# Moving three side tasks of a two-block transformer kernel: weight sums, modulation columns, first values

## The chip, the cores and the metric

The kernel runs on one core of a Trainium2 chip. The metric is the device time of one launch in microseconds (us); the time of a kernel is the median of several runs. The core's engines each run their own instruction queue in order: PE (matrix products), DVE (vector), ACT (scalar, activations), POOL (a second vector engine) and SP (which here only issues DMAs). DMAs are issued from SP's queue and from POOL's queue.

## The reference, cut to what matters

Two blocks over 1024 tokens of 1024 features, all in float32. The first block is attention followed by a feed-forward with a convolution; the second is a gated linear attention over a context of 256 tokens and then the 1024 tokens, followed by an MLP. Both are modulated or normed:

```python
# first block
mix = token_mixer(x, w_in, b_forget, rel_bias, w_out)      # 8 forgetting + 8 band heads
x = layer_norm(ALPHA * x + mix, ln1_g, ln1_b)
u = causal_conv3(x @ w_up) + conv_b                         # 2 x 2816 columns
value, gate = split(u)
ffn = (value * gelu(gate)) @ w_down                         # 2816 -> 1024
x = layer_norm(ALPHA * x + ffn, ln2_g, ln2_b)
# second block, with six modulation vectors of 1024 from c @ ada_w + ada_b:
#   0 shift1, 1 scale1, 2 gate1, 3 shift2, 4 scale2, 5 gate2
h   = modulate(rmsnorm(x, g1), shift1, scale1)
x   = x + gate1 * gla_mixer(context, h)                     # 4 heads, both directions
h   = modulate(rmsnorm(x, g2), shift2, scale2)
x   = x + gate2 * (relu(h @ w1) ** 2) @ w2                  # MLP, 4096 wide
out = rmsnorm(x, g3)
```

## The kernel before, in words

**Products.** A float32 product is three PE matmuls (`mm3`): high by high, high by low, low by high. The two halves of an operand come from `split`: a cast on ACT, then a subtraction on DVE. The large products (the two up and the two down products) use seven block products in place of eight (Strassen-Winograd), so some operands are sums of blocks. The sums of the weights `w_down` are made in `right_sums`: for each of 11 groups it loads two tiles of 512 KB (`sumw`, `sumv`), does four DVE operations of 128x512, and stores both tiles to DRAM (T1T3w, T4T2w). The down pass loads them back as operands.

**Stages, in order of time.** Attention (0 to some 480 us, `attention_phase`); the product with `w_out` and the first norm (`mixed`, to 642); the first up pass with convolution and gate (`up_pass`, `conv_gate`, 642 to 1063, 22 pairs of column blocks); the down pass (`ffn_down`, 1063 to 1352), into which the context's part of the second block (`context`) is mixed; the last norms of the first block and the values of the first head (`norm1`, `first_values`, 1352 to 1400); the gated linear attention (`prepare` and `scan` of four heads, 1400 to 1708); its output gate (`gate_out`, 1708 to 1797); output product, second up pass, second down pass (to 2558).

**What sets the order.** The generators are interleaved by `merge`: it always advances the one that has spent the smallest share of its stated total. From that program order and from priorities (the transposes have a high one) a scheduler fixes each engine's order when the kernel is built; nothing is reordered on the chip. In the attention `merge` mixes the modulation vectors 0 and 1, `down_sums` (all of `right_sums`, with loads and stores on SP's queue) and the attention itself. In the down pass it mixes `most()`, the six first of the seven block products (one step is 12 matmuls), and `context`.

**Modulation.** `ada(v, c, 256, ...)` makes 256 columns of vector v: eight weight tiles of 128 KB (`ada_w`) are loaded, scaled and added on DVE (one operation each, into `ada_acc`), and a matmul sums over the partitions. For v = 2 and 5 the result is stored to DRAM; for v = 3 and 4 it stays. Before, the four vectors 2 to 5 are made in the gated linear attention, 36 steps after each scan, with the weights in the same four buffers (`raw`) through which `w_get` brings the weights of the products.

**Convolution and gate.** `conv_gate` runs after each pair of the up pass: ACT scales the block, DVE adds two shifted copies (L1063, L1064), ACT does the gelu, DVE multiplies. Every second pair it also makes the sums of the left operand of the down pass. The next pair's ACT copy of a block product (L801) overwrites what L1064 has read, and PE reuses the PSUM bank after that copy.

**Scan.** `scan(h)` is a chain over eight tiles: PE makes `att`, `dS` and three `o` matmuls; DVE forms the new state (`Snew`) and, with the root mean square from ACT and POOL, normalises `o` into `res` (L1318), which frees the one bank of `o`. `gate_out` is 768 matmuls (`tokp`) of 128x256.

Of the kernel before, what the change touches and what calls it, by code (L numbers as in the profile page):

```python
# [10 lines left out]
F32 = mybir.dt.float32  # L11
# [6 lines left out]
P = 128  # L18
D = 1024
# [19 lines left out]
def drain(gen):  # L39
    for _ in gen:  # L40
        pass
# [13 lines left out]
def build(tc, I, out, dbg=None, stop=None):  # L55
# [4 lines left out]
    def pool(stack, name, bufs, **kw):  # L60
        return stack.enter_context(tc.tile_pool(name=name, bufs=bufs, **kw))
# [128 lines left out]
    def right_sums(W, n, pl, dst, load, store):  # L190

        w, v = (pl.tile([P, D], F32, tag=x, name=f"sum{x}") for x in "wv")
        for i, t in enumerate((w, v)):
            load.dma_start(out=t.rearrange("p (h c) -> p h c", h=2), in_=W[2 * n + i].rearrange("h p c -> p h c"))
        yield 1
        DVE.tensor_tensor(out=w[:, XS], in0=w[:, YS], in1=w[:, XS], op=ALU.subtract)
        DVE.tensor_tensor(out=w[:, YS], in0=v[:, YS], in1=w[:, YS], op=ALU.subtract)
        yield 1
        DVE.tensor_tensor(out=v[:, YS], in0=v[:, YS], in1=w[:, XS], op=ALU.subtract)
        DVE.tensor_tensor(out=v[:, XS], in0=v[:, XS], in1=v[:, YS], op=ALU.subtract)  # L200
        yield 1
        for x, t in zip(dst, (w, v)):
            store.dma_start(out=x[n], in_=t)
# [8 lines left out]
    def attention_phase():  # L212
# [7 lines left out]
        pp = pool(st, "pp", 5)  # L220
        f1 = pool(st, "f1", 1)
        ar = pool(st, "ar0", 2)
        twp = pool(st, "tw", 1)

        Wqk, Wv = wlist("wqk"), wlist("wv")
        Wv0 = wlist("wv0")
# [315 lines left out]
                except StopIteration:  # L542
                    return

        def down_sums():

            for n in range(NCH // 2):
                yield from right_sums(I["w_down"], n, twp, TW, SP, SP)

        tws = down_sums()  # L550

        def split_y(p):
            kk = (p + 4) % 8
            for c in (slice(0, 512), slice(512, T)):
# [12 lines left out]

        for p in range(8):
            feed[0] = projections(p)
            merge([(some(mod, 13), 13), (some(tws, 5), 5), (until_pair(), attn_cost(p)), (feed[0], 20801 * ((p % 2 == 0) + (p < 7)) + 1), (split_ys(p), 6)])  # L570
        return st

    st = attention_phase()
# [478 lines left out]
    def conv_weights(st):  # L1052
        convc.append(pool(st, "convc", 1, reuse_waits="tile").tile([P, 2 * NCH, 4], F32, name="convc"))
        SP.dma_start(out=convc[0], in_=I["conv"])
        convc.append(pool(st, "sums1", 2, reuse_waits="tile"))

    def conv_gate(n, gv_, gg_, *_):

        o = res[3], res[7]
        for i, (psum, x) in enumerate(zip((gv_, gg_), o)):  # L1060
            c = convc[0][:, 2 * n + i, :]
            ACT.activation(x, psum, AF.Identity, scale=c[:, 2:3], bias=c[:, 3:4])
            DVE.scalar_tensor_tensor(out=x[:, 1:T], in0=psum[:, 0:T - 1], scalar=c[:, 1:2], in1=x[:, 1:T], op0=ALU.mult, op1=ALU.add)  # L1063
            DVE.scalar_tensor_tensor(out=x[:, 2:T], in0=psum[:, 0:T - 2], scalar=c[:, 0:1], in1=x[:, 2:T], op0=ALU.mult, op1=ALU.add)  # L1064
        gelu = ACT.activation(o[1], o[1], AF.Gelu_apprx_tanh)
        if n == NCH - 1:
            exp_tables(gelu)
        if n % 2 == 0:
            even[:] = [convc[1].tile([P, T], F32, tag="g", name="geven")]
            DVE.tensor_tensor(out=even[0], in0=o[0], in1=o[1], op=ALU.mult)  # L1070
            return
        DVE.tensor_tensor(out=o[0], in0=o[0], in1=o[1], op=ALU.mult)
        a, b = convc[1].tile([P, D], F32, tag="s12", name="sums12"), convc[1].tile([P, 512], F32, tag="s4", name="sums4")
        left_sums(even[0], o[0], a, b)
        for x, t in (("A12A22", o[0]), ("A11S3", even[0]), ("S1S2", a)):
            POOL.dma_start(out=left1[x][n // 2], in_=t)
        POOL.dma_start(out=narrow1["S4"][n // 2], in_=b)
# [43 lines left out]
    def ffn_down():  # L1121

        nonlocal hi, lo, rawp, wp
        st, cst = ExitStack(), ExitStack()
        set_banks(st, "f", {"mm": (1, 5, "down"), "c": (1, 2, "z hps fp tokp xtp"), "ct": (1, 1, "ctp ktp dS xtp")}, reuse_waits="tile")
        counts = ("r0", 2), ("l0", 2), ("draw1", 4), ("l1", 4), ("r1", 4), ("rp", 2), ("fc1", 1)
        r0, l0, raw, l1, r1, rp, fc = (pool(st, n, b, reuse_waits="tile") for n, b in counts)
        left, right = in_turn((l0, 2), (l1, 4)), in_turn((r0, 2), (r1, 4))
        rawp, wp = (pool(cst, n, 4, side="right") for n in ("wraw1", "wsplit1"))
        B = blocks(wlist("w_down"), left1, narrow1, TW)  # L1130
        gb = [fc.tile([P, D], F32, name=f"ln2{c}") for c in "gb"]
        junk = fc.tile([P, D], BF16, name="junk")
        mv = [fc.tile([P, 6], F32, name=f"mvd{t}") for t in range(NT)]

        def with_x1(t, c, of):

            x = rp.tile([P, 512], F32, tag="x", name="x1res")
            SP.dma_start(out=x, in_=x1d[t][:, c])
            DVE.scalar_tensor_tensor(out=res[t][:, c], in0=x, scalar=ALPHA, in1=of, op0=ALU.mult, op1=ALU.add)

        def add(o, a, b):
            DVE.tensor_tensor(out=o, in0=a, in1=b, op=ALU.add)

        def complete(t, c, psum):
            i = 0 if c == XS else 1
            add_sum(res[t][:, c], psum, res[t][:, c], mv[t][:, i:i + 1])

        def normed(t):
            layer_norm(res[t], mv[t], *gb, junk)
            SP.dma_start(out=x2d[t], in_=res[t])  # L1150

        def p1(t, p):
            ACT.copy(res[t][:, XS], p)

        def p6(t, p):
            add(res[t + 4][:, XS], p, res[t][:, XS])
            with_x1(t, XS, res[t][:, XS])

        def p2(t, p):
            complete(t, XS, p)  # L1160

        def p5(t, p):
            add(res[t + 4][:, YS], p, res[t + 4][:, XS])
            with_x1(t, YS, res[t + 4][:, YS])
            with_x1(t + 4, YS, res[t + 4][:, YS])

        def p3(t, p):
            complete(t, YS, p)
            with_x1(t + 4, XS, res[t + 4][:, XS])
            normed(t)  # L1170

        def p7(t, p):
            complete(t + 4, YS, p)
            add(res[t + 4][:, XS], p, res[t + 4][:, XS])

        def p4(t, p):
            complete(t + 4, XS, p)
            normed(t + 4)

        def run(a, b, evac, by_tile):  # L1180
            psums = [acc("down") for _ in range(4)]
            for t in block_product(B, raw, left, right, NCH // 2, psums, a, b, by_tile, mm3):
                if t is not None:
                    evac(t, psums[t])
                yield t

        def most():
            for a, b, f in (("A11", "B11", p1), ("S2", "T2", p6), ("A12", "B21", p2), ("S1", "T1", p5), ("S4", "B22", p3), ("S3", "T3", p7)):
                for t in run(a, b, f, 3):
                    yield 2724 if t is None else 2043  # L1190
                if f is p2:
                    bcast(gb[0], "ln2_g")
                    bcast(gb[1], "ln2_b")

        def norm1(t):
            rows(res[t], t, vec["gs1"], vec["sh1"], rms_of(res[t], junk), rp)
            split(by_k(res[t]), hi[:, :, toks(t)], lo[:, :, toks(t)])

        def first_values():

            for t, psum in token_product(Wgv0, hi, lo, NT, HV + 32):
                ACT.copy(v0[t], psum[:, 0:HV])
                DVE.tensor_copy(out=ht[t], in_=psum[:, HV:HV + 32])
                yield

        merge([(most(), 179784), (context(cst), CTXSHARE)])
        cst.close()
        actp = pool(act_st, "act2", 1, side="right")
        rawp, wp = pool(st, "wraw2", 4), pool(st, "wsplit2", 4)
        hi, lo = (actp.tile([P, KD, T], F32R, name=n) for n in ("act2_hi", "act2_lo"))  # L1210
        values = first_values()
        ready = deque(range(4))
        for t in run("A22", "T4", p4, 3):
            if ready:
                norm1(ready.popleft())
        for t in range(4, NT):
            norm1(t)
        drain(values)
        st.close()
# [107 lines left out]
    ac = pool(gla_st, "ac", 1)  # L1327

    def modulation():
        for v in (2, 4, 3, 5):  # L1330
            for c in range(0, D, 256):
                yield from ada(v, c, 256, None, ac)

# [2 lines left out]
    for h in range(4):  # L1336
        scan(h)
        if h < 3:
            prepare(h + 1)
        for _ in range(36):  # L1340
            next(mod, None)
    for h in range(4):
        gate_out(h)
# [270 lines left out]
```

## Time and profile before

| | us |
|---|---|
| median of 3 runs (2556.66 to 2559.73) | 2557.68 |
| the profiled execution | 2559.18 |
| its span in the trace | 2557.5 |
| PE busy | 2425.3 (95%) |
| DVE busy | 1744.9 (68%) |
| ACT busy | 1260.3 (49%) |

How to read it: the span is the trace's time from the first to the last instruction; the profiled execution is 1.7 us longer than its span and 1.5 us longer than the median. PE is busy nearly all the time, so the time that can be had lies in the stages where it is not, and the tables of stages below show which these are. A granted clock of 1.00 is full speed of PE (2.4 GHz), and PE at its lower level runs at half of that.

### The profile page before, as it was taken

The page shows a single profiled execution, that of the slowest core. Times are in us where ns is not written, and L with a number is a line of the kernel's source. Part 1 is how long each engine was busy: PE and PEld are TensorE (multiplying, and loading weights), DVE is VectorE, ACT ScalarE, POOL GpSimd, SP SyncE. Part 2 cuts the span into 40 slices and gives each one's busy share as a digit, 9 for nine tenths or more (in the row PEclk, how much of TensorE's full clock was granted, in tenths as well). Part 3 has the DMA queues.
Part 4 walks back from the last instruction along what each step waited for, and adds up shares of the span by engine and source line. Part 5 has one row for each costly group of instructions (what it writes and reads, how often), then busy time and mean ns, then how long its engine had stood idle before and what let it go on. Part 6 is the DMA issues. An engine that isn't in the chain of part 4 may idle for free. (4 is left out here: it accounts for less than half of the span.)

```text
span 2557.5 us, 37112 instructions
## 1 busy us (share of the span) xinstructions
PE 2425.3 (95%) x12822; PEld 2066.3 (81%) x12822; DVE 1744.9 (68%) x3299; ACT 1260.3 (49%) x2284; POOL 445.6 (17%) x677
## 2 busy tenths in 40 slices
PE   8999999998999999899997989979999999999998
PEld 7788989777888888678887878869788878878886
DVE  6876666658788888667585876652578777555456
ACT  4555556735555554565364543322355555544443
POOL 4675742421000000100022000000011111100000
PEclk9989999999999999899999999989999999999999
DMA  8653322353223322476652222231436777576565
GB/s 281 228 183 96 98 84 60 98 168 111 90 87 116 108 90 95 148 239 199 200 184 76 64 88 88 63 122 34 148 124 226 276 271 273 202 240 209 196 208 189
DMA packets 189085, 387.24 MB, mean 151 GB/s; under 512 B 22296, under 2 KB 54680, under 8 KB 188896
## 3 DMA queue, kind: packets, MB, share of 16 engines
q1 hardware_dynamic: 168032, 310.14, 37.0%
q0 software_dynamic: 20864, 74.72, 7.9%
q8 instruction: 101, 1.65, 0.3%
q14 instruction: 88, 0.72, 0.1%
HBM read 275.95 MB, written 100.43 MB: 147 GB/s over the span
## 5 line engine op out<-in xcount | busy, mean ns | idle before, releaser
L103 DVE TENSOR_TENSOR dpart<-draw,dpart 128x512 fp32r<-128x512 f32 x378 | 250.6, 693 | 183.2 <-ACT dpart L102 175.9
L102 ACT CAST dpart<-draw 128x512 fp32r<-128x512 f32 x378 | 221.5, 620 | 243.5 <-PE Y L131 65.7
L130 PE MATMUL s<-act_hi,uh 128*128 128x512 f32 (+1 forms) x640 | 244.0, 381 | 1.0 <-ACT res L805 1.0
L131 PE MATMUL s<-act_lo,uh 128*128 128x512 f32 (+1 forms) x640 | 243.3, 380 | 0.0
L132 PE MATMUL s<-act_hi,ul 128*128 128x512 f32 (+1 forms) x640 | 243.2, 380 | 0.0
L601 POOL TENSOR_TENSOR rstd<-rstd,mhalf 128x1 f32<-128x1 f32 x74 | 54.8, 744 | 926.7 <-DVE rstd L600 734.4
L130 PE MATMUL tokp<-wh,act_hi 128*128 128x256 f32 (+1 forms) x512 | 148.3, 292 | 0.0
L394 ACT ACTIVATE P<-P,mx 128x640 f32<-128x640 f32 (+7 forms) x128 | 94.4, 738 | 108.9 <-DVE mx L391 86.6
L132 PE MATMUL tokp<-wh,act_lo 128*128 128x256 f32 (+1 forms) x512 | 147.6, 289 | 0.0
L131 PE MATMUL tokp<-wl,act_hi 128*128 128x256 f32 (+1 forms) x512 | 147.2, 289 | 0.0
L130 PEld LDWEIGHTS s<-act_hi,uh 128*128 128x128 f32 x640 | 121.7, 190 | 24.1 <-ACT res L805 1.5
L131 PEld LDWEIGHTS s<-act_lo,uh 128*128 128x128 f32 x640 | 121.7, 190 | 22.2
L132 PEld LDWEIGHTS s<-act_hi,ul 128*128 128x128 f32 x640 | 121.5, 190 | 22.4
L396 POOL TENSOR_SCALAR P<-P,mx 128x640 f32<-128x640 f32 (+7 forms) x128 | 94.7, 743 | 183.2 <-DVE mx L395 166.5
L130 PE MATMUL s<-ext_8hi,uh 128*128 128x512 f32 (+1 forms) x320 | 121.2, 379 | 1.4 <-ACT res L809 1.4
L131 PE MATMUL down<-dpart 128*128 128x512 f32 x308 | 121.7, 396 | 0.4 <-DVE dpart L103 0.2
L131 PE MATMUL s<-ext_8lo,uh 128*128 128x512 f32 (+1 forms) x320 | 121.2, 379 | 0.6 <-DVE ext_8lo L103 0.6
L132 PE MATMUL s<-ext_8hi,ul 128*128 128x512 f32 (+1 forms) x320 | 121.1, 378 | 0.0
L132 PE MATMUL down<-dpart 128*128 128x512 f32 x308 | 120.9, 393 | 0.0
L102 ACT CAST uh<-res 128x1024 fp32r<-128x1024 f32 x80 | 83.0, 1040 | 77.0 <-PE s L131 61.4
L130 PE MATMUL down<-dpart 128*128 128x512 f32 x308 | 117.7, 395 | 2.2 <-ACT dpart L102 2.2
L103 DVE TENSOR_TENSOR ul<-res,uh 128x1024 fp32r<-128x1024 f32 x80 | 96.5, 1207 | 26.5 <-ACT uh L102 26.1
(373 smaller groups left out, 7174.9 us busy)
## 6 DMA issues: line engine op xcount, KB each, us to landing
ada_w<-in_ada_w SPq DMA_DIRECT2D x192, 128.0 KB, 2.2
res<-in_w_up SPq DMA_DIRECT2D x44, 512.0 KB, 3.3
res<-in_mlp_w SPq DMA_DIRECT2D x32, 512.0 KB, 4.3
draw<-in_mlp_w SPq DMA_DIRECT2D x48, 256.0 KB, 3.7
draw<-in_w_down SPq DMA_DIRECT2D x33, 256.0 KB, 3.3
raw<-in_wqk SPq DMA_DIRECT2D x32, 256.0 KB, 3.4
sumw<-in_mlp_w SPq DMA_DIRECT2D x16, 512.0 KB, 6.6
sumv<-in_mlp_w SPq DMA_DIRECT2D x16, 512.0 KB, 6.6
```

The source lines that it names most:

```text
L102: ACT.copy(h, raw)
L103: DVE.tensor_tensor(out=l, in0=raw, in1=h, op=ALU.subtract)
L130: PE.matmul(out=o, lhsT=ah, rhs=bh, start=first, stop=False, **kw)
L131: PE.matmul(out=o, lhsT=ah, rhs=bl, start=False, stop=False, **kw)
L132: return PE.matmul(out=o, lhsT=al, rhs=bh, start=False, stop=last, **kw)
L394: ACT.activation(Pm[:, 0:W], Pm[:, 0:W], AF.Exp, bias=mx[:, 0:1], scale=-1.0, accum_out=mx[:, 1:2])
L396: POOL.tensor_scalar(out=Pm[:, 0:W], in0=Pm[:, 0:W], scalar1=mx[:, 2:3], scalar2=0.0, op0=ALU.mult, op1=ALU.add)
L601: POOL.tensor_tensor(out=t[:, 1:2], in0=t[:, 0:1], in1=mhalf, op=ALU.pow)
```

## The change

It touches six places.

A. `down_sums` and its pool are taken out of the attention.

B. The same sums are made in the first up pass: `conv_gate` calls `right_sums` at every even pair, 11 times, placed behind the pair's last load. Loads are on SP's queue, stores on POOL's. The pool for them has one buffer, and the old pool of two buffers is split into two pools of one.

C. The six first steps of `most()` are taken before the context is mixed in; the stated total of the rest is smaller by the same.

D. Modulation vectors 2 and 5 are made in the down pass, as a third generator, with two buffers of their own for the weights; their matmul uses the bank of the context's transposes ("ct").

E. A step of `first_values` (24 matmuls) is taken before each of the last four norms.

F. In the gated linear attention only vectors 4 and 3 remain, with 18 steps after each scan in place of 36.

```diff
@@ attention_phase
-        def down_sums():
-            for n in range(NCH // 2):
-                yield from right_sums(I["w_down"], n, twp, TW, SP, SP)
-        tws = down_sums()
...
-            merge([(some(mod, 13), 13), (some(tws, 5), 5), (until_pair(), attn_cost(p)), (feed[0], 20801 * ((p % 2 == 0) + (p < 7)) + 1), (split_ys(p), 6)])
+            merge([(some(mod, 13), 13), (until_pair(), attn_cost(p)), (feed[0], 20801 * ((p % 2 == 0) + (p < 7)) + 1), (split_ys(p), 6)])
@@ conv_weights, conv_gate
-        convc.append(pool(st, "sums1", 2, reuse_waits="tile"))
-
-    def conv_gate(n, gv_, gg_, *_):
+        convc.extend(pool(st, n, b, reuse_waits="tile") for n, b in (("even1", 1), ("sums1", 1)))
+
+    def conv_gate(n, gv_, gg_, last):
...
         if n % 2 == 0:
+            with tc.issue_after(last.ins):
+                drain(right_sums(I["w_down"], n // 2, convc[2], TW, SP, POOL))
             even[:] = [convc[1].tile([P, T], F32, tag="g", name="geven")]
@@ ffn_down
-        set_banks(st, "f", {"mm": (1, 5, "down"), "c": (1, 2, "z hps fp tokp xtp"), "ct": (1, 1, "ctp ktp dS xtp")}, reuse_waits="tile")
+        set_banks(st, "f", {"mm": (1, 5, "down"), "c": (1, 2, "z hps fp tokp xtp"), "ct": (1, 1, "ctp ktp dS ada xtp")}, reuse_waits="tile")
...
+        ar, ac = pool(cst, "ar", 2, side="right"), pool(cst, "ac", 1, side="right")
...
-        merge([(most(), 179784), (context(cst), CTXSHARE)])
+        def modulation():
+            for v in (2, 5):
+                for c in range(0, D, 256):
+                    yield from ada(v, c, 256, ar, ac)
+
+        products = most()
+        for _ in range(6):
+            next(products)
+        merge([(products, 163440), (context(cst), CTXSHARE), (modulation(), 72)])
...
         for t in range(4, NT):
+            next(values)
             norm1(t)
@@ gated linear attention
-            for v in (2, 4, 3, 5):
+            for v in (4, 3):
...
-        for _ in range(36):
+        for _ in range(18):
             next(mod, None)
```

What this does to the order on the engines, at three places.

DVE around the first pair of the up pass, after the change. L103 are the splits whose results (`act_lo`, `ext_4lo`, `ext_8lo`, `ul`) PE reads; L704 to L708 form the blocks to split; L1022 and L1024 end a norm; L196 to L200 are the weight sums.

```order
L103 TENSOR_TENSOR act_lo<-res_6921,act_hi 128x8x128
L707 TENSOR_TENSOR res_6920<-res_6920,t_7721 128x512
L103 TENSOR_TENSOR ext_4lo<-t_7721,ext_4hi 128x4x128
L196 TENSOR_TENSOR sumw<-sumw 128x512
L103 TENSOR_TENSOR act_lo<-res_6924,act_hi 128x8x128
L103 TENSOR_TENSOR ext_8lo<-res_6920,ext_8hi 128x8x128
L704 TENSOR_TENSOR res_6921<-res_6925,res_6921 128x512
L705 TENSOR_TENSOR t_7826<-res_6925,res_6921 128x512
L708 TENSOR_TENSOR res_6925<-res_6925 128x512
L197 TENSOR_TENSOR sumw<-sumv,sumw 128x512
```

The same place before (the lines of that code are 8 higher there: L712 is L704).

```order
L103 TENSOR_TENSOR act_lo<-res_7035,act_hi 128x8x128
L715 TENSOR_TENSOR res_7034<-res_7034,t_7835 128x512
L103 TENSOR_TENSOR ext_4lo<-t_7835,ext_4hi 128x4x128
L103 TENSOR_TENSOR act_lo<-res_7038,act_hi 128x8x128
L103 TENSOR_TENSOR ext_8lo<-res_7034,ext_8hi 128x8x128
L712 TENSOR_TENSOR res_7035<-res_7039,res_7035 128x512
L713 TENSOR_TENSOR t_7940<-res_7039,res_7035 128x512
```

The rows of after are the second of two whole sums that stand here; the first one's four operations stand in the eleven rows ahead. So eight operations on loaded tiles now stand among the splits of the first pair.

ACT at the start of the down pass, after the change. `dpart` are the casts of the down product's operands, `wh` those of the context's weights, `ctx_x` and `ctx_f` the context's norm and modulation, between which PE transposes (`ctp`).

```order
L614 ACTIVATE ctx_f,ss<-ctx_x 128x1024
L102 CAST wh<-raw 128x576 x2
L102 CAST dpart<-draw 128x512 x2
L935 ACTIVATE ctx_x<-ctx_x,rstd 128x1024
L1057 ACTIVATE res_6925<-res_6925 128x1024
L86 ACT_TABLE_LOAD
L102 CAST wh<-raw 128x576
L631 ACTIVATE ctx_f<-ctp,v_shc,v_gsc 128x128 x4
L102 CAST wh<-raw 128x576 x4
L631 ACTIVATE ctx_f<-ctp,v_shc,v_gsc 128x128 x4
L102 CAST wh<-raw 128x576
L102 CAST dpart<-draw 128x512
```

The same place before.

```order
L622 ACTIVATE ctx_f,ss<-ctx_x 128x1024
L102 CAST wh<-raw 128x576 x2
L102 CAST dpart<-draw 128x512
L102 CAST wh<-raw 128x576
L943 ACTIVATE ctx_x<-ctx_x,rstd 128x1024
L1065 ACTIVATE res_7039<-res_7039 128x1024
L86 ACT_TABLE_LOAD
L102 CAST dpart<-draw 128x512
L102 CAST wh<-raw 128x576
L639 ACTIVATE ctx_f<-ctp,v_shc,v_gsc 128x128 x4
L102 CAST dpart<-draw 128x512
L639 ACTIVATE ctx_f<-ctp,v_shc,v_gsc 128x128 x4
```

The context's first norm stands where it stood, behind the first casts of the down product; four casts of the context's weights now stand between the two groups of its modulation, where one `dpart` stood. On PE the context's first eight transposes and 24 `tokp` follow two steps of the down product (24 matmuls) in both kernels.

PE in the last scan, after the change: `dS`, `att` and `o` belong to the scan, `tokp` (L130 to L132) to the output gate.

```order
L130 MATMUL tokp<-wh,act_hi 128x256
L131 MATMUL tokp<-wl,act_hi 128x256
L1296 MATMUL dS<-v,ktok 128x256
L132 MATMUL tokp<-wh,act_lo 128x256
L1313 MATMUL o<-Sin,eq 128x256
L1314 MATMUL o<-Snew,eq 128x256
L1315 MATMUL o<-v,asum 128x256
L130 MATMUL tokp<-wh,act_hi 128x256
```

The same place before; the last row is the first of the output gate's.

```order
L1309 MATMUL o<-Snew,eq 128x256
L1310 MATMUL o<-Snew,eq 128x256
L1311 MATMUL o<-v,asum 128x256
L164 MATMUL ada<-ada_acc,ones 128x256
L1309 MATMUL o<-Sin,eq 128x256
L1310 MATMUL o<-Snew,eq 128x256
L1311 MATMUL o<-v,asum 128x256
L164 MATMUL ada<-ada_acc,ones 128x256
L130 MATMUL tokp<-wh,act_hi 128x256 x2
```

Ahead of the first row and behind the last one stand more `tokp`: most spaces between the groups of `dS`, `att` and `o` of the last scan hold 7 to 38 of them. Before, all of them stood behind the last `o` and the last `ada`.

## Rows read from the trace of the kernel before

**Rows 1.** The page: busy time, share and instructions of each engine.

```profile
PE 2425.3 (95%) x12822; PEld 2066.3 (81%) x12822; DVE 1744.9 (68%) x3299; ACT 1260.3 (49%) x2284; POOL 445.6 (17%) x677
```

**Rows 2.** Busy time by stretch; first column start and end, then length.

```profile
core 0: us, PE busy (x) PEld busy (x) DVE busy (x) ACT busy (x) POOL busy (x), PEclk, DMA share, GB/s
20.00:180.00 160.00, 146.47 (x881) 128.30 (x880) 122.11 (x293) 79.87 (x185) 102.54 (x150) 0.96 0.71 237
180.00:480.00 300.00, 299.18 (x2000) 268.01 (x1999) 198.24 (x548) 168.37 (x377) 145.43 (x228) 1.00 0.29 82
600.00:642.00 42.00, 31.17 (x153) 25.65 (x152) 38.24 (x61) 22.93 (x34) 5.71 (x8) 0.92 0.34 121
642.00:1063.00 421.00, 419.54 (x1908) 349.38 (x1907) 338.16 (x385) 213.19 (x263) 21.41 (x40) 1.00 0.27 95
1063.00:1092.00 29.00, 16.93 (x66) 13.12 (x66) 20.56 (x30) 21.24 (x38) 5.59 (x8) 0.76 0.83 266
1092.00:1300.00 208.00, 205.59 (x1035) 173.44 (x1035) 143.43 (x290) 111.25 (x225) 13.49 (x11) 1.00 0.63 207
1352.00:1400.00 48.00, 34.47 (x255) 33.70 (x254) 27.24 (x55) 22.45 (x45) 13.13 (x12) 0.89 0.20 72
1400.00:1660.00 260.00, 246.18 (x1430) 214.27 (x1428) 181.85 (x474) 110.39 (x257) 14.53 (x24) 0.99 0.24 75
1660.00:1708.00 48.00, 31.12 (x122) 22.78 (x123) 33.55 (x89) 12.35 (x32) 4.77 (x8) 0.83 0.50 155
1708.00:1800.00 92.00, 91.53 (x763) 91.32 (x762) 21.56 (x44) 20.02 (x46) 0.00 (x0) 1.00 0.10 32
```

**Rows 3.** PE's waits, 20 to 180 us: total us, times, longest.

```profile
PE S L386 <- DVE mx L391: 7.2, 8, 1.4
```

**Rows 4.** Tiles sumw and sumv: one operation, and DVE's idle time for loads.

```profile
L196 DVE TENSOR_TENSOR sumw<-sumw x11: 683/693/1283, 20.8 to 165.8; 128x512 f32<-128x512 f32 x11
...
  DMA sumw<-in_w_down: 14.1, 6
...
  DMA sumv<-in_w_down: 10.5, 7
```

**Rows 5.** DMA issues: queue, count, KB each, median us from issue to landing.

```profile
sumv<-in_w_down SPq DMA_DIRECT2D x11, 512.0 KB, 4.5
...
T4T2w<-sumv SPq DMA_DIRECT2D x11, 512.0 KB, 4.4
...
S1S2g<-sums POOLq DMA_DIRECT2D x11, 512.0 KB, 3.0
```

**Rows 6.** PE's waits, 600 to 642 us.

```profile
PE xtp L91 <- DVE res L1032: 4.4, 1, 4.4
PE s L130 <- ACT res L801: 3.4, 1, 3.4
```

**Rows 7.** Timeline in one pair of the up pass: start, us, engine, line.

```profile
799.90 0.59 ACT L801 COPY res<-s 128x512 f32<-128x512 f32 x1 [0.78 <-DVE res L1064]
...
801.77 0.39 PE L130 MATMUL s<-ext_4hi,uh 128*128 128x512 f32 x1
```

**Rows 8.** Timeline of PE at the start of the down pass.

```profile
1075.78 0.66 PE L91 MATMUL ctp<-ident,ctx_x 128*128 128x128 f32 x4 [3.11 <-ACT ctx_x L943]
1080.64 1.11 PE L91 MATMUL ctp<-ident,ctx_x 128*128 128x128 f32 x4 [4.20 <-ACT ctx_f L639]
```

**Rows 9.** Timeline of PE at the last norms of the first block.

```profile
1363.87 4.46 PE L693 MATMUL xtp<-diag,res 128*128 128x128 f32 x24 [11.62 <-DVE rstd L600]
1369.67 2.05 PE L693 MATMUL xtp<-diag,res 128*128 128x128 f32 x16 [1.35 <-DVE res L703]
```

**Rows 10.** PE's waits, 1660 to 1708 us, and the modulation's DVE operation.

```profile
PE o L1309 <- DVE res L1318: 8.7, 6, 4.2
PE ada L164 <- DVE ada_acc L160: 3.0, 1, 3.0
...
L160 DVE SCALAR_TENSOR_TENSOR ada_acc<-ada_w,cs,ada_acc x112: 467/483/486, 1444.2 to 1702.7; 128x256 f32<-128x256 f32 x112
```

More of the change, by code (lines that the diff above doesn't have):

```diff
@@ L222, in attention_phase @@
         ar = pool(st, "ar0", 2)
-        twp = pool(st, "tw", 1)
         Wqk, Wv = wlist("wqk"), wlist("wv")
@@ L1072, in conv_gate @@
         DVE.tensor_tensor(out=o[0], in0=o[0], in1=o[1], op=ALU.mult)
-        a, b = convc[1].tile([P, D], F32, tag="s12", name="sums12"), convc[1].tile([P, 512], F32, tag="s4", name="sums4")
+        a, b = convc[2].tile([P, D], F32, tag="s12", name="sums12"), convc[2].tile([P, 512], F32, tag="s4", name="sums4")
         left_sums(even[0], o[0], a, b)
```

## The prediction

> **What bounds the kernel now.** First the page's engine row: PE is busy 95% of the span, DVE 68%, ACT 49% [rows 1]. So the end is set by PE nearly everywhere, and a change can win only where PE idles or runs at its lower clock. The table of stages shows where. In the attention behind 180 us, in the up pass and in the output gate PE idles 0.8, 1.5 and 0.5 us: nothing is to be had there. It idles 13.5 us (160 less 146.5) in the attention's first 160 us, 10.8 around the first norm, 12.1 at the start of the down pass, 13.5 in the norms and values, 13.8 in the linear attention to 1660, and 16.9 in its last 48 us [rows 2]. The clock column adds to this: 0.96, 0.92, 0.76, 0.89, 0.99 and 0.83 there, against 1.00 in the full stages. The change touches each of these stages, and it puts work into the two, up and down pass, that have no idle time. So I cost each part against the idle time of its own stage. The sum is made for the profiled execution, 2559.2 us.
>
> **A, sums out of the attention.** 44 DVE operations of 0.69 us (30 us) leave a stretch in which DVE is busy 122 of 160 us; so do DVE's standstills for their loads, 14.1 + 10.5 us [rows 2, 4]. DVE queues in order, so whatever stands behind such a standstill waits too; PE's largest wait in the stretch is for DVE's row maxima, 7.2 us in 8 waits [rows 3]. With some 55 us of DVE time free, the maxima come in time. The idle time of 13.5 us and the lost clock (4% of 160, 6.4 us) bound the gain at -19. I take -13, near the idle time; the projections' start needs its own loads, so not all goes. Ends -19 and 0 (0 if the maxima wait for PE's own logits).
>
> **B, sums in the up pass.** Two places.
> At the start, the order puts two whole sums, eight operations or 5.5 us, among the splits that PE needs. DVE is busy 38.2 of 42 us there, and PE already waits 4.4 us for L1032 and 3.4 for L801 [rows 2, 6]. The second sum's load needs the first one's stores, with the nearest landings 4.4 and 4.5 us [rows 5]; some 9 us of other DVE work stand between, so it should be in time. Some of the eight stand behind the last operand that PE lacks. I take +4; ends 0 (all behind what PE needs) and +10 (5.5, and one landing of 4.5 not covered).
> Then nine sums, one each two pairs (a pair is 421/22 = 19.1 us). DVE goes from 338 to 338 + 9 x 2.8 = 363 of 421 us: still free on average. But three of the four operations stand ahead of the convolution's last addition, upon which L801 waits. L801 ended at 800.49 and PE needed its bank at 801.77 [rows 7]: slack 1.3 us, and three operations take up to 3 x 0.69 = 2.1. So up to 0.8 each, 7 in all; DVE's own idle moments take some of it. I take +2; ends 0 and +7.
>
> **C, six products' steps ahead of the context.** This should let the down product run until the context's norm is ready, in place of PE's 3.1 and 4.2 us waits for it [rows 8]. But the order shows that PE's context transposes still stand behind only two steps, since they have high priority. On ACT four casts of context weights now stand between the two halves of the context's modulation, where one of the down operands stood, and the down casts come later. So I take no gain, and +2 for the later down operands (about three casts moved past). Ends -10 (the waits go, of 12.1 idle) and +8 (both waits lengthened by as much again).
>
> **D, modulation 2 and 5 in the down pass.** 64 DVE operations of 0.48 us (31 us) [rows 10], 64 loads of 128 KB on SP and 8 matmuls. DVE is busy 143 of 208 us there [rows 2]; with the share of the load, 31 over some 240 us, it reaches 82%, as in the up pass, where PE still runs without a gap. The matmuls cost about 1 us of PE that was as much in the linear attention, so nothing on balance. The loads stand ahead of the down operands' own on SP; four buffers of those cover it. In the order the early norms' transposes come later, since their memory is free only after the modulation, and some ACT casts slide into the last norms' chain. I take +2; ends 0 and +8 (a quarter of the 31 us shows).
>
> **E, values between the last norms.** PE stands 11.6 us before the norms' first 24 transposes and runs these at 0.186 us each, against 0.128 for the next 16 [rows 9]. Afterwards 17 value matmuls stand ahead of the last norms' first transposes; at 0.12 us for 256 columns (92 us over 763, [rows 2]) and so 0.135 for 288, that is 2.3 us of the wait filled. The wait of 1.35 goes too, and the clock's share, 24 x 0.058 = 1.4. Sum -5. Ends -13 (all idle time of the stage) and +3 (the norm's chain is pushed by the casts of D).
>
> **F, half the modulation, and gate products in the last scan.** In the last 48 us PE waits for L1318 and for the modulation's own sums, 8.7 and 3.0 us [rows 10], and in all it idles 16.9 us and loses about 5 to the lower clock (31.1 busy at a mean of 0.83, [rows 2]): 22 us. DVE, busy 33.6 of 48, has some 20 us of `ada` there, of which half stays. Now gate products stand between the scan's groups: 7 to 38 matmuls, 0.8 to 4.6 us, against waits of up to 4.2. I take -18. In 1400 to 1660 there are 13.8 us idle and 1% of 260 us of clock: 16; half the DVE load of modulation goes and there is no new filling but what slides forward, so -6. Together -24; ends -10 and -38.
>
> **Sum.** -13 + 4 + 2 + 2 + 2 - 5 - 24 = -32. 2559.2 - 32 = 2527.2; the median of the runs is 1.5 lower than the profiled one, so 2526.
>
> **A rule against the change.** The stores of the sums move from SP's queue to POOL's. In the up pass, with DVE busy 338 of 421 us, POOL's stores of the same size landed in 3.0 us, not later than SP's in the attention, 4.4 [rows 2, 5]; so I give no price to the move. The Trainium skill, page "SBUF — State Buffer", section "SBUF: two separate sides", warns that a DMA from the GpSimd queue can starve while DVE runs an operation of its two-port mode, since its descriptors aren't written meanwhile, and advises the SP or ACT queue. By it the sum would be about -22 and not -32; the trace speaks against it here.
>
> **Rivals.**
> 1. The gate products don't fill the last scan: their weights' casts and loads queue behind the scan's work, so PE, in order, waits at them instead. For it: in-order queues, and the weights share four buffers with the modulation. Against: half of that modulation is gone. Then F gives -6 and not -24: 2526 + 18 = 2544.
> 2. C does what it says: the context's norm is done while the down product runs. Against: the order on PE. Then C is -10 and not +2: 2514.
> 3. POOL's stores wait for DVE. At the start the first sum's stores land one pair (19 us) later, less the 9 us of other work, so the second sum stands 10 us in front of PE's splits: +10, 2536. Against: the 3.0 us above. This is what the rule of the Trainium skill above would do here.
> 4. Slower: the sums' loads make DVE stand in the up pass, where PE has no slack but 1.3 us. SP queues them behind the pair's own loads, and the single buffer frees only after POOL's stores. Each us that DVE stands, in each of 11 sums, goes to PE. Without B's +6 the sum is -38; the four operations keep +4; so the kernel is slower than before from a mean standstill of 34/11 = 3.1 us. In the attention it was (14.1 + 10.5)/11 = 2.2 [rows 4], which gives -34 + 25 = -9. With a whole landing of 4.5 us each [rows 5] it is -34 + 50 = +16: 2574. Against: the next sum is two pairs, 38 us, away, and DMA is busy 27% there against 71% in the attention.
>
> **How the numbers follow.** Forecast 0.68, rival 1 0.13, rival 2 0.06, rival 3 0.04, rival 4 0.09. The range goes from 2500 (A, E and F towards their ends, -6, -3 and -6, with rival 2's -12) to 2548 (rival 1 with +4 more in B): it leaves out rival 4 and some 0.1 of sums in which several ends meet. A measurement of this kernel can tell about 0.2%, 5 us, from no change. Faster by more: all cases but rival 4, less 0.01 for rival 1 with the high ends, 0.90; rival 4 splits into 0.05 within 5 us (mean standstills of 2.7 to 3.5) and 0.05 slower.
>
> **What would show it.** A: PE waits for L391 nearly gone and PE busy over 150 of the first 160 us. B: PE's wait around 640 grows by some 4 us, and waits at L801 every second pair stay under 0.5; DVE's idle time for `sumw` and `sumv` in the up pass under 1 us a sum. C: the waits for `ctx_x` and `ctx_f` still there. D: no waits of `down` for DVE. E: the 11.6 us wait down to about 9, with values ahead of it. F: the last scan with PE busy over 90%. The forecast is wrong if the up pass is over 10 us longer, or if the scan's PE waits move to the gate weights.

## The result

The changed kernel takes 2516.6 us in the median of 4 runs (2514.8 to 2520.8), against 2558.7 for the kernel before in the same comparison; the ratio is 0.9838, with a 95% interval of 0.9821 to 0.9855. So it is some 42 us (1.6%) faster; 32 were forecast. The profiled execution of after has a span of 2513.2 us, 44.3 less than before.

Where the time went is read from the first and last matmul of each kind. The table gives the length of each stage so marked, each column from one profiled execution; the columns e1 to e12 are the experiments below. The last line is the median of the runs of each kernel.

| stage, us | before | after | e1 | e2 | e3 | e4 | e5 | e6 | e7 | e8 | e9 | e10 | e11 | e12 |
|---|---|---|---|---|---|---|---|---|---|---|---|---|---|---|
| attention (to first `sq`) | 525.7 | 506.3 | 524.2 | 506.0 | 507.3 | 505.7 | 507.0 | 509.7 | 505.6 | 506.3 | 506.6 | 507.4 | 507.8 | 523.7 |
| w_out (to first `s`) | 108.6 | 107.7 | 105.5 | 110.5 | 109.1 | 107.8 | 108.3 | 108.3 | 109.1 | 104.9 | 107.5 | 106.9 | 106.2 | 107.0 |
| up pass (to first `down`) | 430.5 | 439.4 | 429.5 | 441.9 | 442.2 | 443.4 | 443.3 | 434.8 | 446.0 | 430.3 | 430.9 | 430.3 | 433.0 | 430.8 |
| down pass (to last `down`) | 287.1 | 297.3 | 297.4 | 306.9 | 280.9 | 295.7 | 283.5 | 293.2 | 298.3 | 300.2 | 284.0 | 293.1 | 285.7 | 286.0 |
| norms, values, first head (to first `o`) | 117.6 | 114.9 | 114.9 | 114.2 | 113.4 | 123.5 | 113.4 | 114.9 | 113.5 | 115.0 | 112.5 | 112.3 | 117.2 | 120.4 |
| scans and gate (to last `tokp`) | 328.6 | 287.8 | 288.1 | 286.2 | 332.4 | 292.5 | 319.5 | 286.5 | 286.5 | 287.7 | 290.6 | 289.3 | 332.1 | 301.0 |
| rest | 759.4 | 759.8 | 760.6 | 760.4 | 763.3 | 761.8 | 757.2 | 764.7 | 759.6 | 759.4 | 764.8 | 761.0 | 758.3 | 757.6 |
| whole kernel, median | 2558.7 | 2516.6 | 2523.6 | 2528.0 | 2543.0 | 2530.3 | 2532.4 | 2507.2 | 2519.9 | 2505.5 | 2496.4 | 2505.0 | 2544.7 | 2530.0 |

From before to after: -19.4 in the attention, -0.9 at the product with w_out, +8.9 in the up pass, +10.2 in the down pass, -2.7 in the norms, -40.8 in scans and gate, +0.4 in the rest, which the change doesn't touch: -44.3. Stages that an experiment doesn't touch differ by 2 to 6 us from kernel to kernel; the up pass (439.4 to 446.0 with the sums as in after), the down pass (293.2 to 300.2 with C and D as in after) and the rest (757.2 to 764.8) by 7 to 8. Smaller differences are not read, and where several kernels share a stage all of them are compared. The profiled execution of e3 is the slowest of its four, 7 us above their median.

Busy time of each engine in after, by stage (columns as in [rows 2]):

```profile
20.00:180.00 160.00, 156.40 (x1044) 142.66 (x1044) 111.82 (x289) 88.90 (x208) 107.95 (x179) 0.99 0.35 99
...
614.00:1053.00 439.00, 426.37 (x1934) 352.70 (x1932) 369.59 (x437) 216.94 (x273) 32.57 (x61) 0.99 0.40 143
1053.00:1080.00 27.00, 14.66 (x56) 11.55 (x56) 22.83 (x35) 19.04 (x35) 5.01 (x8) 0.68 0.99 355
1080.00:1351.00 271.00, 264.61 (x1303) 222.23 (x1304) 204.33 (x431) 143.03 (x280) 22.95 (x16) 0.98 0.69 225
1351.00:1400.00 49.00, 38.95 (x280) 37.61 (x279) 34.07 (x71) 28.92 (x59) 12.31 (x13) 0.90 0.20 70
1400.00:1708.00 308.00, 299.92 (x1888) 271.84 (x1887) 196.80 (x502) 129.94 (x304) 18.43 (x31) 0.99 0.19 59
1708.00:1754.00 46.00, 45.67 (x381) 45.46 (x379) 9.76 (x22) 8.66 (x22) 0.55 (x1) 1.00 0.05 17
```

Against [rows 2], PE's idle time in the attention's first stretch falls from 13.5 to 3.6 us and its clock is back; the linear attention has 8.1 us idle in 308, where 30.7 were idle before. The up pass now has more gaps: 12.6 us in 439, where before, from its first matmul on, 5.9 were idle in 430:

```profile
634.00:1064.00 430.00, 424.15 (x1935) 353.74 (x1933) 347.02 (x396) 219.17 (x272) 21.41 (x40) 0.99 0.28 96
```

### The profile page after: what moved, and what is told of

Read it like the earlier page. It is cut to its first block, busy times and chain, and to the rows that moved or that the text cites. A ratio compares the mean times of both kernels' runs of the same rounds, so it can differ in the third digit from the quotient of the medians.

```text
span 2513.2 us, 37123 instructions
## 1 busy us (share of the span) xinstructions
PE 2407.7 (96%) x12822; PEld 2062.3 (82%) x12822; DVE 1749.1 (70%) x3299; ACT 1259.7 (50%) x2284; POOL 448.3 (18%) x699
## 5 line engine op out<-in xcount | busy, mean ns | idle before, releaser
L103 DVE TENSOR_TENSOR dpart<-draw,dpart 128x512 fp32r<-128x512 f32 x378 | 249.6, 691 | 164.8 <-ACT dpart L102 162.9
L130 PE MATMUL s<-act_hi,uh 128*128 128x512 f32 (+1 forms) x640 | 243.8, 381 | 1.6 <-ACT res L797 1.6
L132 PE MATMUL s<-act_hi,ul 128*128 128x512 f32 (+1 forms) x640 | 243.0, 380 | 0.0
L130 PE MATMUL tokp<-wh,act_hi 128*128 128x256 f32 (+1 forms) x512 | 148.9, 293 | 1.1 <-ACT wh L102 1.1
L132 PE MATMUL tokp<-wh,act_lo 128*128 128x256 f32 (+1 forms) x512 | 147.6, 290 | 0.0
L130 PEld LDWEIGHTS s<-act_hi,uh 128*128 128x128 f32 x640 | 121.5, 190 | 24.7 <-ACT res L797 2.2
L132 PEld LDWEIGHTS s<-act_hi,ul 128*128 128x128 f32 x640 | 121.2, 189 | 22.4
L132 PE MATMUL down<-dpart 128*128 128x512 f32 x308 | 122.4, 397 | 0.0
L130 PE MATMUL down<-dpart 128*128 128x512 f32 x308 | 118.9, 400 | 2.7 <-ACT dpart L102 2.6
L132 PE MATMUL s<-ext_8hi,ul 128*128 128x512 f32 (+1 forms) x320 | 121.3, 379 | 0.0
L130 PE MATMUL s<-ext_8hi,uh 128*128 128x512 f32 (+1 forms) x320 | 121.2, 379 | 0.0
L103 DVE TENSOR_TENSOR ul<-res,uh 128x1024 fp32r<-128x1024 f32 x80 | 96.5, 1208 | 22.2 <-ACT uh L102 22.2
```

What stands on the lines that cost most here:

```text
L103: DVE.tensor_tensor(out=l, in0=raw, in1=h, op=ALU.subtract)
L130: PE.matmul(out=o, lhsT=ah, rhs=bh, start=first, stop=False, **kw)
L132: return PE.matmul(out=o, lhsT=al, rhs=bh, start=False, stop=last, **kw)
```

## The experiments

**A: the sums in the attention.** e1 takes A and B back.

```diff
-            with tc.issue_after(last.ins):
-                drain(right_sums(I["w_down"], n // 2, convc[2], TW, SP, POOL))
...
+        def down_sums():
+            for n in range(NCH // 2):
+                yield from right_sums(I["w_down"], n, twp, TW, SP, SP)
```

> The changed kernel with A and B undone: the weight sums are made in the attention again (loads and stores on SP's queue) and not in the up pass. Theory 1 (the sums' standing DVE in the attention cost PE 19 us there, and cost 9 us in the up pass): the first product with w_out starts near 525 us instead of 506, the up pass is about 430 us long instead of 439, total near 2527. Rival (the attention's gain came from something else that moved with it): w_out starts within 5 us of 506, and the total falls to about 2508.

Measured: 2523.6 us (ratio to before 0.9853, 0.9835 to 0.9871). The attention is 17.9 us longer again, the up pass 9.9 shorter, w_out 2.2 shorter (within its spread): theory 1. e11 goes into the cause. It is the kernel before, without the four `DVE.tensor_tensor` lines of `right_sums`.

> The kernel before, with the four DVE operations of each weight sum left out in the attention; loads and stores stay (so the down product reads unsummed weights). With the sums there the attention ended (first product with w_out) at 525.7 us, without them at 506.3. Theory 1a (DVE's operations and its standing for their loads delay the row maxima): near 507 to 510. Theory 1b (the 23 MB of traffic, or SP's queue, delay the attention's own loads): 518 or later.

The attention ends at 507.8 us although the loads and stores are all there. PE's largest wait from 20 to 180 us in e1, then in after, and the same stretch of e11 by engines:

```profile
PE S L386 <- DVE mx L391: 5.1, 5, 1.3
```

```profile
PE proj L130 <- DVE X L236: 1.4, 1, 1.4
```

```profile
20.00:180.00 160.00, 153.85 (x1034) 139.83 (x1033) 106.18 (x287) 89.60 (x208) 105.42 (x178) 1.00 0.74 243
```

In e11 the DMA moves 243 GB/s, as before (237 in [rows 2]), and PE runs 1034 matmuls in the stretch, as after (1044), where before it ran 881. So it was DVE, by its operations and by standing for their loads, and not the traffic or SP's queue: theory 1a. The two parts of DVE's time weren't separated.

**B: the sums in the up pass.** e6 leaves the same four lines out of after; e8 holds them behind the gate's multiplication.

```diff
-            with tc.issue_after(last.ins):
-                drain(right_sums(I["w_down"], n // 2, convc[2], TW, SP, POOL))
+            ws = right_sums(I["w_down"], n // 2, convc[2], TW, SP, POOL)
+            with tc.issue_after(last.ins):
+                next(ws)
...
-            DVE.tensor_tensor(out=even[0], in0=o[0], in1=o[1], op=ALU.mult)
+            m = DVE.tensor_tensor(out=even[0], in0=o[0], in1=o[1], op=ALU.mult)
+            with tc.issue_after(m.ins):
+                drain(ws)
```

> The changed kernel with the four DVE operations of each weight sum left out; their loads and stores stay (so the down product reads unsummed weights). The up pass took 439 us after the change, 430 with the sums in the attention. Theory 5a (DVE's operations ahead of the convolution's additions make PE wait at the block copies): up pass 429 to 431. Theory 5b (the traffic or the queues of the sums' DMAs cost): 437 or more.

> The changed kernel with the same sums, but their four DVE operations are held behind the gate's multiplication and so stand no longer ahead of the convolution's additions. Theory 5a with place (not their number, but where they stand costs): PE's waits for the first block copy fall from 9.7 us to under 5, up pass 430 to 433, total near 2510. Rival (DVE's load as such costs: 416 operations in 421 us): up pass 437 or more.

PE's waits at the ACT copies of the up pass, in before, after, e6 and e8 (its line differs by kernel: L801 of before is L793 in after and e8, and L787 in e6):

```profile
PE s L130 <- ACT res L801: 3.9, 2, 3.4
```

```profile
PE s L130 <- ACT res L793: 9.7, 11, 3.9
```

```profile
PE s L130 <- ACT res L787: 7.0, 2, 6.0
```

```profile
PE s L130 <- ACT res L793: 3.5, 3, 2.3
```

e8 settles it: with all 44 operations there, but in another place, the up pass takes 430.3 us and the kernel 2505.5 (ratio 0.9796, 0.9766 to 0.9826). e6 came out between its two expectations, at 434.8. Two waits are left in it, one of 6.0 us; from the first matmul with `ext_4`, behind the start, to the first `down` it takes 424.7 us, against 431.8 in after and 423.0 before. So behind the start it agrees with 5a; up to there it takes 10.1 us against 7.7 in after, which wasn't followed further. The path in after, on DVE, ACT and PE (timelines):

```profile
663.35 0.69 DVE L197 TENSOR_TENSOR sumw<-sumv,sumw 128x512 f32<-128x512 f32 x1
664.07 0.69 DVE L199 TENSOR_TENSOR sumv<-sumv,sumw 128x512 f32<-128x512 f32 x1
664.68 1.28 DVE L1055 SCALAR_TENSOR_TENSOR res<-res,convc,res 128x1023 f32<-128x1023 f32 x1
665.88 0.68 DVE L200 TENSOR_TENSOR sumv<-sumv 128x512 f32<-128x512 f32 x1
666.48 1.22 DVE L103 TENSOR_TENSOR ul<-res,uh 128x1024 fp32r<-128x1024 f32 x1
667.61 1.28 DVE L1056 SCALAR_TENSOR_TENSOR res<-res,convc,res 128x1022 f32<-128x1022 f32 x1
```

```profile
668.98 0.58 ACT L793 COPY res<-s 128x512 f32<-128x512 f32 x1 [2.17 <-DVE res L1056]
```

```profile
669.62 0.50 PE L130 MATMUL s<-ext_4hi,uh 128*128 128x512 f32 x1 [1.37 <-ACT res L793]
```

DVE has no gap in this pair; L197, L199 and L200 stand ahead of L1056, ACT's copy waits for it, and PE 1.37 us for the copy.

**C and D: the down pass.** e2 takes C back (the merge begins at the first step), e3 takes D and F back (all modulation in the linear attention, in the shared buffers), e7 gives the modulation weights eight buffers.

```diff
-        for _ in range(6):
-            next(products)
-        merge([(products, 163440), (context(cst), CTXSHARE), (modulation(), 72)])
+        merge([(products, 179784), (context(cst), CTXSHARE), (modulation(), 72)])
```

> The changed kernel with C undone: the context is mixed in from the first step of the down pass. The down pass took 297 us from first to last matmul after the change and 287 before. Theory 2a (C lengthens the start: more loads and casts of the context stand ahead of the down operands): down pass near 290, total near 2510. Theory 2b (D, the modulation, lengthens it): down pass stays at 295 to 299, total within 3 us of 2517.

> The changed kernel with D and F undone: all four modulation vectors are made in the linear attention, 36 steps after each scan, through the four buffers shared with the weights. Theory 2b: the down pass falls to about 289; 2a: it stays near 297. For the linear attention and output gate (403 us from the last down matmul to the last gate product after the change, 446 before): theory 3 (everything gained there but a few us hangs on F): 440 or more, total near 2550. Rival (E, or the moved values, gave much of it): under 430, total near 2535.

> The changed kernel with eight buffers, not two, for the modulation weights in the down pass. There the modulation lengthens the down pass by 16 us (297 against 281 with the modulation elsewhere), and DVE stands 19 us for these loads. Theory 6a (DVE standing for the loads is what costs): DVE's wait for them under 5 us and the down pass 283 to 288, total near 2505. Theory 6b (the 64 operations, the loads' place on SP's queue, or the DMA traffic cost): down pass 294 to 300, total near 2517.

e2 is slower, not faster: 2528.0 us, the down pass 9.6 longer. So C is a gain beside D, of 9.6 us against after (7 to 14 against the five kernels with C and D as in after). Without D it is at most small: e3, e5 and e9, with C, take 280.9, 283.5 and 284.0 us, and before, e11 and e12, without it, 287.1, 285.7 and 286.0. D beside C costs 14 us in the mean of these kernels (9 to 19 from pair to pair; 16.4 for after against e3), and without C 20 (e2 against before). Theory 2a is wrong. Of 2b it holds that D is what lengthens the pass, but by more than the 8 us that it gave, with C hiding part of it; so it missed e2 too. The down pass's first 40 us and its rest in after, e3 and e7:

```profile
1053.00:1093.00 40.00, 26.65 (x101) 21.39 (x102) 29.49 (x46) 27.33 (x51) 6.30 (x10) 0.70 0.90 316
1093.00:1351.00 258.00, 252.61 (x1259) 212.39 (x1259) 197.67 (x420) 134.74 (x263) 21.67 (x14) 0.99 0.69 224
```

```profile
1059.00:1099.00 40.00, 29.76 (x123) 23.82 (x122) 27.43 (x41) 28.67 (x54) 7.27 (x10) 0.79 0.89 303
1099.00:1340.00 241.00, 241.00 (x1231) 206.26 (x1230) 175.54 (x357) 133.95 (x265) 19.65 (x16) 1.00 0.62 198
```

```profile
1061.00:1101.00 40.00, 20.98 (x83) 16.75 (x82) 27.61 (x44) 25.76 (x48) 6.47 (x10) 0.70 0.90 307
1101.00:1359.00 258.00, 255.04 (x1283) 215.79 (x1282) 202.90 (x425) 137.13 (x269) 19.95 (x14) 1.00 0.70 224
```

What C gains lies behind the start: in e3 PE hasn't a gap in 241 us. What in the new order brings it wasn't separated. D costs in both parts: 22 matmuls fewer in the first 40 us (22 x 0.23, the spacing of two `down` matmuls in the timeline, is 5 us), and 5.4 us idle and a clock of 0.99 behind. There DVE stands for the modulation weights, here in after from 1053 to 1352 us:

```profile
DVE ada_acc L160 <- DMA ada_w<-in_ada_w: 19.3, 18, 3.1
```

In e7 DVE no longer stands for them. The idle time behind the start falls to 3.0, and 24 more matmuls fit into the same 258 us (24 x 0.23 = 6 us); but the first 40 us run only 83 matmuls, with PE waiting for the context's norm. That wait, and how long the context's two tiles took to land, in after and in e7:

```profile
PE ctp L91 <- ACT ctx_x L935: 12.0, 2, 8.1
```

```profile
DMA to landing us min/median/max: 3.7/5.3/6.9
```

```profile
DMA to landing us min/median/max: 3.6/6.4/9.1
```

So the down pass stays at 298.3 (2519.9 in all), and neither theory alone holds: more buffers let more of these loads go ahead at the start, where DMA is busy 90% of the time already, and what is won behind is lost there. In SP's queue 13 modulation loads stand ahead of the context's second tile in e7, and 6 in after; the tile is asked for 18 and 15 us after the first `down`, and lands after 9.1 and 6.9 us. That fits a delay by the loads; no run holds them back alone, so it isn't shown. By the 24 matmuls behind the start, DVE's standing is worth an estimated 6 of D's 14 to 16 us; 5 more lie at the start, and the rest stays open.

**E: values between the norms.** e4 leaves out the `next(values)` line.

> The changed kernel with E undone: the values' products follow the last norms again. Theory 4 (values between the norms fill a few us of PE's wait for the norms' chain): the stretch from the last down matmul to the first scan output is 118 us in place of 114.9, total 3 to 5 us longer, near 2521. Rival (nothing gained, the chain of the norms sets the end of the stretch): within 1 us of 114.9, total near 2517.

Measured: 2530.3 us. The stretch to the first `o` is 123.5 us, 8.6 longer, and the scans and the gate 4.7 longer. PE at the last norms in after, then e4:

```profile
1360.57 0.40 PE L91 MATMUL hps<-ident,res 128*32 128x128 f32 x1 [5.38 <-DVE rstd L592]
1365.03 3.76 PE L685 MATMUL xtp<-diag,res 128*128 128x128 f32 x16 [4.07 <-DVE rstd L592]
```

```profile
1368.42 7.26 PE L685 MATMUL xtp<-diag,res 128*128 128x128 f32 x40 [14.59 <-DVE diag L676]
```

The wait of 11.6 us of [rows 9] would have become 14.6 and is now 5.4 and 4.1. Why the later scans gain too wasn't tested.

**F: the linear attention.** e5 is e3 with two buffers of its own for the modulation weights, e9 the same with eight (and e8's sums), e12 the kernel before with nothing else changed than these eight.

```diff
-    ac = pool(gla_st, "ac", 1)
+    ar, ac = pool(gla_st, "ar", 8), pool(gla_st, "ac", 1)
...
-                yield from ada(v, c, 256, None, ac)
+                yield from ada(v, c, 256, ar, ac)
```

> As the run with the modulation back in the linear attention, but its weights have two buffers of their own and do not share the four of the product weights. The DVE operations are the same 128. Theory 3a (the gate products were held back by the order in which four shared buffers are handed round, and filling the last scan is what pays): the last scan is filled, 403 to 412 us from the last down matmul to the last gate product, total near 2514 if the down pass falls to 289. Theory 3b (the DVE time of the modulation is what held PE): over 425 us, total near 2540.

> All four modulation vectors in the linear attention, with eight buffers of their own (two in the run before of this kind, where DVE stood 56 us for these loads and the stretch from the last down matmul to the last gate product took 433 us); the weight sums behind the gate's multiplication. Theory 3c (DVE standing for the loads is what cost there): DVE's standstill for these loads under 10 us and the stretch 405 to 415; with the down pass near 283, total near 2502. Theory 3b (the 31 us of DVE operations themselves cost): stretch 425 or more, total 2515 or more.

> The kernel before with one thing changed: the modulation weights in the linear attention have eight buffers of their own, not the four of the product weights. Nothing is moved to another stage. The stretch from the last down matmul to the last gate product was 446.2 us before. Theory 3c (the shared buffers held both the gate products and DVE; the number of modulation operations there costs nothing): stretch 403 to 410, the last scan filled, total near 2518. Theory 3d (the other parts of the change are needed for it, E or the earlier values above all): 420 or more, total 2532 or more.

From the last `down` to the last `tokp`: before 446.2 us, after 402.7, e3 445.8, e5 432.9, e9 403.1, e12 421.4. DVE's standing for the modulation weights from 1400 us on, in before and in e5, and the standing of all engines for them over the whole kernel in e9:

```profile
DVE ada_acc L160 <- DMA ada_w<-in_ada_w: 11.4, 18, 1.4
```

```profile
DVE ada_acc L160 <- DMA ada_w<-in_ada_w: 55.6, 52, 3.0
```

```profile
  DMA ada_w<-in_ada_w: 6.5, 4
```

e3 has all of after but D and F, and is back at the time of before: so the gain hangs on F. Where the buffers are shared, the first gate product stands right behind the last `ada` matmul: at 1703.9 us behind 1703.8 in before, 1691.0 behind 1690.4 in e3, and in after 1639.2 behind 1637.8, ahead of the last scan. With buffers of its own for the modulation the gate products begin 46 to 62 us before the modulation ends (e5, e9, e12). So in e5 they fill the last scan, but DVE stands 55.6 us for weights with only two buffers, and 30 of the 43 us are missing. In e9, with eight, DVE doesn't stand for them at all (the 6.5 us are POOL's, in the attention). There 120 of the 128 DVE operations of the modulation are in the linear attention (the first eight already run in the down pass), and the stretch is as short as in after, where 64 are. So their number costs nothing there; what cost was the buffers, in before because they were shared (DVE stood only 11.4 us), in e5 because they were too few. Shared buffers in a larger number weren't run. e12 is between its expectations: the buffers alone bring 25 us to this stretch of the kernel before (2530.0 in all, ratio 0.9890, 0.9874 to 0.9907). By e4 13 more belong to E; 5 are not accounted for.

**A version that is faster than both.** e9 leaves the down pass free of all but eight modulation operations (284.0 us), has the sums at the better place (430.9) and the filled scans: 2496.4 us, ratio to before 0.9753 (0.9731 to 0.9775). e10 was another way: the sums as in e8, vector 2 in the down pass, vector 5 beside the output gate (`ada(5, ...)` after each `gate_out(h)`, four buffers).

> The weight sums behind the gate's multiplication, and modulation vector 5 made beside the output gate (four buffers of its own), where DVE is busy 20% and PE 99%; only vector 2 stays in the down pass. Theory 6c (half of the 16 us that the modulation costs the down pass go, and beside the output gate it costs nothing): down pass near 290, stretch from the last down matmul to the last gate product within 3 us of 403, total near 2497. Rival (the cost comes with the first loads, however many follow): down pass 297 or more, total near 2505.

Measured: 2505.0 us. Vector 5 cost nothing beside the gate (401.6 to the last `tokp`). The down pass is 293.1, between the two expectations: 7.1 shorter than in e8, but not than in e6 (293.2), which has all of D. In the medians the kernel is no faster than e8 (2505.5), as the rival has it. So it isn't shown that half of D's work saves half of its cost.

## Why the prediction was right or wrong

The direction and the range held. The sum of -32 is made of terms that were off by up to 17 us. A, the start of B, and F came out better than forecast by 28 us together, the steady part of B, C with D, and E worse by 15; that the total was only some 12 us off is in part luck.

- **What bounds the kernel.** Right: the gains came only in stretches where PE was idle or slow, the losses in the two stages that were full.
- **A, -13 forecast, -19.4 measured.** The mechanism held (the wait of [rows 3] is gone from after's list). Its size was the bound (13.5 + 6.4 is 19.9, where I wrote 19), not the middle: I kept 6 us back for the projections' own loads and the clock, and e11 shows that the clock came back with the waits (1.00).
- **B, start: +4 forecast.** -0.9 against before, +2.2 against e1, neither clear of the spread of this stage. The second sum's load was not quite in time: DVE stood 1.4 us for it, at 621 us.
- **B, steady: +2 forecast, +8.9 measured, end +7.** The path was the right one (L801 of before), the term too small. I let DVE's idle moments take most of the 0.8 us per sum; the pair shown has none there, and all of L197, L199 and L200 ahead of the last addition. From 640 us on the waits for this copy are 5.8 us of the 8.9; the rest wasn't traced. e8 shows that it was the place. The five other kernels with the same up pass (e2 to e5, e7) have it 11 to 16 us longer than before, beyond the 10 at which the prediction called itself wrong.
- **C, +2 forecast, -10 measured beside D (e2), about -4 without it.** The step that failed: I read the order at the pass's start, found the context's first transposes where they were, and took no gain for the whole part. At the start there is none (123 matmuls in the first 40 us in e3, 129 before); the gain lies in the part behind (241 us in e3, 247 before), at which I had not looked.
- **D, +2 forecast, +14 to +16 measured, end +8.** I priced the operations as DVE load (82% busy, which PE would bear) and the loads as covered. Both steps failed: DVE stood 19.3 us for these loads with two buffers, a mechanism that I had priced in A, and the pass's start ran 22 matmuls fewer. e7, without that standing, is no shorter, so it is not the whole cost. C and D together, +4 against +10.2, look better than they were.
- **E, -5 forecast.** The stage fell by 2.7 net. e4 shows that within the change E is worth 8.6 there and 13 in all: without it the wait for the norms' chain is 14.6 us, where it was 11.6 before. That D pushed the chain back, as the +3 end had it, would fit this but wasn't tested.
- **F, -24 forecast, -40.8 measured, end -38.** The filling was right and the sum too careful. PE in the last scan and shortly ahead of it, in before and in after (there from the first gate product):

```profile
1643.00:1708.00 65.00, 47.46 (x236) 37.23 (x236) 40.44 (x110) 17.49 (x45) 5.87 (x10) 0.87 0.42 129
1639.00:1708.00 69.00, 68.83 (x505) 66.32 (x506) 30.42 (x77) 25.64 (x65) 5.81 (x10) 1.00 0.14 44
```

The 22 us of idle time and clock of the last scan, of which the sum left 4, went whole. The sum's other part, 6 of 16 us ahead of it, counted only idle time and clock. The idle time fell by 4 us (6.2 from the first `o` to 1639, 9.9 in the same length before), but PE ran 1038 matmuls there and not 967: products of the heads themselves moved forward, some 11 us (71 x 0.16) for which the sum had no term. With these, 37 of the 41 us are accounted for. The cause that I named beside the filling, half of the DVE load, isn't needed: e9.

- **Rivals.** 1 didn't come: the last scan has no PE waits. 2 came in its size beside D, at another place. 4 didn't: DVE stood once, the 1.4 us at the start, for all the sums' loads. 3 didn't: POOL's stores in the up pass, beside DVE busy 84%, landed as before from SP (2.9 and 4.4, [rows 5] for the second):

```profile
T1T3w<-sumw POOLq DMA_DIRECT2D x11, 512.0 KB, 2.9
T4T2w<-sumv POOLq DMA_DIRECT2D x11, 512.0 KB, 3.1
```

The warning in the Trainium skill, page "SBUF — State Buffer", section "SBUF: two separate sides", that DMAs from the GpSimd queue starve beside DVE's two-port operations, did not show in this stage. Whether any of the stage's DVE operations runs in that mode the profile doesn't say, so the rule itself isn't tested here.

## What to carry to other kernels

A side task on an engine that works in order isn't priced by its busy time alone. Ask first whether the engine stands for the task's loads (e5 against e9), whether the task stands ahead of an operation that another engine waits for (after against e8), and what its loads delay in a stage whose DMA is busy (e7 points to this). Moving the task to another stage takes these costs along, and D paid for it; here more buffers (e9) and another place in the same stage (e8) were worth more than that move. And where buffers are handed round in a fixed order, look at who else draws from them: here that kept the gate products out of the last scan.

## What the runs showed of the hardware

Traffic alone was harmless where I had thought it might not be: in e11 23 MB of loads and stores more than in after ran between 20 and 180 us of the attention (243 GB/s against 99), and the attention took 507.8 us against 506.3.
